# Modulation vectors of layer 1 and of keys/values: column pairs replaced by whole matrix rows, and all weights in one packed tensor

## The chip, the cores and the metric

One core of a Trainium2 chip runs the whole program. The metric is device time in microseconds (us), median of three runs. TensorE (PE) multiplies matrices, VectorE (DVE), ScalarE (ACT) and GpSimd (POOL) work on tiles of 128 partitions, and SyncE (SP) issues the loads, which 16 DMA engines carry out.

## The reference

A decoder trunk of two layers on 256 positions of width 1024, all in float32. Every sub-layer normalizes its input and then modulates it with vectors computed from one condition vector `c`:

```python
cs = jax.nn.silu(c)
shift, scale, gate = jnp.split(cs @ mod_w[layer] + mod_b[layer], 3, axis=-1)
h = _modulate(_rmsnorm(x, norm_g[layer]), shift, scale)   # h * (1 + scale) + shift
# layer 0: u, g = split(h @ w_in); conv of width 4; two gates; scan; y * silu(g); @ w_out
# before layer 1, keys and values from the residual x after layer 0:
shift, scale = jnp.split(cs @ kv_mod_w + kv_mod_b, 2, axis=-1)
h = _modulate(_rmsnorm(x, kv_norm_g), shift, scale)
k, v = jnp.split(h @ w_kv, 2, axis=-1)
# layer 1: q, g = split(h1 @ w_in); causal attention inside one block; o * silu(g); @ w_out
x = x + gate[:, None, :] * y
```

The products of `cs` with the modulation matrices are vector by matrix: for layer 1's shift and scale, and for those of keys and values, a matrix of 1024 x 2048 (8 MB) is read once each, and 2048 numbers come out.

## The kernel before, in words

**Weights.** Every weight comes in blocks of 512 KB into a ring of 11 raw buffers (`NRAW`), in the order of the table `ORDER`. A block takes the buffer of the block 11 places ahead of it, once all users of that one are done. Names: `s`, `m0` are modulation of layer 0 (`m0h` shift, `m0c` scale), `mk` of keys/values, `m1` of layer 1, `g0`/`g1` the gates; `wu`, `wga`, `wgc` the input projection of layer 0, `wo` its output; `wv`, `wka`, `wkb` values and keys; `wgb`, `wqa`, `wqb` gate path and queries of layer 1; `wp` its output.

**Float32 products.** A weight block is split into a high and a low part (`_hi` by a cast on ACT or DVE, `_lo` by a subtraction on DVE), as is the activation, and three fast products (hi·hi, hi·lo, lo·hi) replace one exact one (`mm3`).

**Modulation.** `mod_pair` takes two tiles of 128 outputs at once (a "pair"). `gemv` runs four products at a time, one in each quadrant of 32 columns of the array: shift and scale, even and odd rows, with `cs` repeated over 32 columns (`csB`) as the stationary side. For `mk` all eight row tiles go through PE: 4 rounds of 4 products for a pair. For `m1` row tiles 2 to 7 are summed on DVE (`mac`, `ON_DVE`) and the sum goes through PE with a stationary side of ones: 2 rounds. The profile counts every one of these float32 products as two MATMULs. The row vectors then go to SBUF (`part`, a copy), become columns by two products with `sel2` (`mc`), and get bias and gain on DVE (`sg4`); `mod_apply` uses them on `x1T`, the transposed normalized x.

**The order of the work.** All instructions are recorded and `Plan` places them engine by engine with a list schedule on rough costs, with random changes to the priorities that are kept where its planned end does not suffer. Each engine then runs its list in order. So any change of costs or of program text can move instructions anywhere. Around the change the sequence is: output projection of layer 0 (`r_wo`, lines 851 to 883), residual and root mean square (`resid`, `rms`, `xn_b`), transposition (`tp_b` to `x1T`), `mod_apply` with `mk`, values and keys (`v`, `k`, `pj_wkb`), `mod_apply` with `m1`, gate path and queries (`g`, `q`, `pj_wqb`), attention, output projection (`r_wp`).

Of the kernel before, what the change touches and what calls it, by code (L numbers as in the profile page):

```python
# [44 lines left out]
class Plan:  # L45
    """Records a program and issues it in the order of a list schedule.

    Instructions are recorded in program order with the regions they read and write; what
    they must wait for follows from that and from the buffers of each tag.  They are then
    placed engine by engine by the length of work that still hangs on them, with rough  # L50
    costs, and issued in the order of their planned starts."""
# [109 lines left out]
        # the buffers of a tag are taken over in turn, once all uses of the last tile are done  # L161
# [47 lines left out]
    # a list schedule: of what can start about now, each engine takes what is most urgent  # L209
    def _forward(self, urge):  # L210
# [12 lines left out]
        while len(seq) < n:  # L223
# [61 lines left out]
    def order(self):  # L285
# [14 lines left out]
        # shaken priorities are kept where they do no harm  # L300
# [51 lines left out]
def kernel(ctx: ExitStack, tc: tile.TileContext, x, c, mod_w, mod_b, norm_g,  # L352
                       rg_w_in, rg_conv_w, rg_conv_b, rg_w_a, rg_b_a, rg_w_x, rg_b_x,
                       rg_lambda, rg_w_out, kv_norm_g, kv_mod_w, kv_mod_b, w_kv,
                       att_w_in, att_w_out, final_norm_g, out):
# [17 lines left out]
    w_in, w_out = rg_w_in[0], rg_w_out[0]  # L373
    aw_in, aw_out = att_w_in[0], att_w_out[0]

    # ------------------------------------------------------------------ streamed loads
    def rows(w, kt0, n):
        return w[kt0 * P:(kt0 + n) * P, :].rearrange("(k p) n -> p k n", p=P)

    def cols(w, c0, n):  # L380
        return w[:, c0:c0 + n].rearrange("(k p) n -> p k n", p=P)

    loads = []

    def want(name, shape, *src):
        loads.append((name, shape, src))

    def want_cols(nm, w, c0, qs=(0, 1)):
        for q in qs:
            want(f"{nm}_{q}", [P, 4, 256], cols(w[q * 512:(q + 1) * 512], c0, 256))  # L390

    def want_rows(nm, w, k0=0, k1=KT):
        for k in range(k0, k1):
            want(f"{nm}_{k}", [P, D], w[k * P:(k + 1) * P, :])

    def want_pair(nm, w, i):
        want(f"{nm}_{i}", [P, 2, 512], rows(w, 2 * i, 2))

    def want_out(nm, w, qs=(0, 2)):
        for q in qs:  # L400
            for n in range(2):
                for r in (q, q + 1):
                    want_pair(f"{nm}{n}", w[:, n * 512:(n + 1) * 512], r)

    def want_mod(nm, w, i):
        for q in range(2):
            for x, c0 in (("h", 0), ("c", D)):
                want_cols(f"{nm}{x}{i}", w, c0 + i * 256, (q,))

    def want_block(b):  # L410
        nm, i = b[:-1], int(b[-1])
        if nm == "s":
            want(f"m0h0_{i}", [P, KT, P], cols(mod_w[0], i * P, P))
            want(f"m0c0_{i}", [P, KT, P], cols(mod_w[0], D + i * P, P))
        elif nm in ("m0", "m1"):
            want_mod(nm, mod_w[i_of[nm]], i)
        elif nm == "mk":
            want_mod(nm, kv_mod_w, i)
        elif nm in ("wu", "wv", "wgb"):
            w, c0 = {"wu": (w_in, 0), "wv": (w_kv, D), "wgb": (aw_in, D)}[nm]  # L420
            want_rows(nm, w[:, c0:c0 + D], i, i + 1)
        elif nm in ("wga", "wka", "wqa"):
            w, c0 = {"wga": (w_in, D), "wka": (w_kv, 0), "wqa": (aw_in, 0)}[nm]
            want_pair(nm, w[:, c0:c0 + 512], i)
        elif nm in ("wgc", "wkb", "wqb"):
            w, c0 = {"wgc": (w_in, D), "wkb": (w_kv, 0), "wqb": (aw_in, 0)}[nm]
            want_cols(f"{nm}{i}", w, c0 + 512 + i * 256)
        elif nm in ("gax", "wgax"):
            want(b, [P, 4, 256], *(w[0, i].rearrange("(k p) n -> p k n", p=P) for w in (rg_w_a, rg_w_x)))
        elif nm in ("g0-", "g1-"):  # L430
            want_rows(nm[:2], mod_w[int(nm[1])][:, 2 * D:], 4 * i, 4 * i + 4)
        else:
            want_out(nm, {"wo": w_out, "wp": aw_out}[nm], (2 * i,))

    i_of = {"m0": 0, "m1": 1}
    for b in ORDER.split():
        want_block(b)
    weights = [l[0] for l in loads if l[0][0] == "w"]
# [629 lines left out]
```

## Time and profile before

| | us |
|---|---|
| median of three runs | 271.81 (271.41 to 272.17) |
| span of the profiled execution, first to last instruction | 269.5 |
| PE busy | 254.6 (94%) |
| DVE busy | 212.2 (79%) |
| ACT busy | 145.6 (54%) |
| read from HBM | 70.87 MB |

The profile has no total of its own for the profiled execution beside the span; the median of the runs is 2.3 us above that span. In the views below, all times count from the first instruction. A row of the chain of waits is a piece of the path that ended last; a row of the timeline is an instruction, or several alike in a row.

### The profile page before, as it was taken

To read this page: it belongs to the slowest core of one execution; us is meant where nothing else is said; L and a number is where in the kernel's file an instruction comes from. 1 tells how busy PE (TensorE), PEld (TensorE's weight loads), DVE (VectorE), ACT (ScalarE), POOL (GpSimd) and SP (SyncE) were. 2 spreads that over 40 slices of the span, in tenths; PEclk is the share of its full clock that TensorE was granted. 3 is DMA by queue.
4 is the path that set the end of the run, shared out by engine and by line. 5 is a ranking of instruction groups with operands and counts; after the bars stand their busy time and mean duration, and the time that the engine had idled before them with its cause. 6 is when DMAs were issued, how large, how long until landed. Compare 5 with 4: busy or idle time off the path is not lost.

```text
span 269.5 us, 5236 instructions
## 1 busy us (share of the span) xinstructions
PE 254.6 (94%) x1987; PEld 222.9 (83%) x1987; DVE 212.2 (79%) x427; ACT 145.6 (54%) x278; POOL 18.2 (7%) x31
## 2 busy tenths in 40 slices
PE   8788999999999799989999999999999999999980
PEld 8675887999799586866887898898899999888870
DVE  3652873869988999897677995997777999998783
ACT  7531740778599793585322252764163629894142
POOL 8100000000030200000000000000010000006120
PEclk9999999999999999999999999999999999999996
DMA  6999999998599985769979999899999692000003
GB/s 210 313 351 379 362 366 384 358 406 322 180 333 358 371 257 182 273 183 349 334 244 359 348 279 306 290 304 389 359 391 378 195 362 88 1 4 1 0 13 142
DMA packets 50968, 72.26 MB, mean 268 GB/s; under 512 B 2792, under 2 KB 37888, under 8 KB 50944
## 3 DMA queue, kind: packets, MB, share of 16 engines
q1 hardware_dynamic: 50112, 71.15, 78.1%
q0 software_dynamic: 688, 0.59, 0.7%
q8 instruction: 15, 0.25, 0.4%
q10 hardware_dynamic: 144, 0.20, 0.2%
q14 instruction: 9, 0.07, 0.1%
HBM read 70.87 MB, written 1.05 MB: 267 GB/s over the span
## 4 chain that ended last, share of the span: by engine, by line
PE 83%; SPq 5%; DMA 4%; DVE 4%; ACT 2%; issue 1%; DVEq 0%
PE g L332 9%; PE v L332 8%; PE r_wo L332 8%; PE r_wp L332 8%; PE u L332 7%; SPq L332 5%; PE pj_wkb L332 4%; PE k L332 4%; PE pj_wgc L332 4%; PE pj_wqb L332 4%; PE q L332 4%; PE ga L332 4%; DMA wga<-in_rg_w_in_dram 4%; PE gvm L332 3%; PE gvmk L332 3%; PE sc L332 2%
## 5 line engine op out<-in xcount | busy, mean ns | idle before, releaser
L332 PE MATMUL g<-h_hi,wgb_hi 128*128 128x256 f32 x64 | 18.4, 288 | 0.0
L332 PE MATMUL g<-h_lo,wgb_hi 128*128 128x256 f32 x64 | 18.3, 287 | 0.0
L332 PE MATMUL g<-h_hi,wgb_lo 128*128 128x256 f32 x64 | 18.1, 283 | 0.0
L332 PE MATMUL u<-h_lo,wu_hi 128*128 128x256 f32 x64 | 18.1, 291 | 0.0
L332 PE MATMUL u<-h_hi,wu_lo 128*128 128x256 f32 x64 | 17.8, 286 | 0.0
L332 ACT ACT_TABLE_LOAD x13 | 16.7, 1283 | 0.9 <-PEq L1054 0.7
L94 ACT COPY partm<-gvm 128x256 f32<-128x256 f32 x7 | 2.6, 373 | 26.0 <-PE gvm L332 26.0
L332 PE MATMUL u<-h_hi,wu_hi 128*128 128x256 f32 x64 | 15.9, 284 | 0.7 <-ACT h_hi L94 0.7
L332 PE MATMUL r_wp<-wp_hi,o_hi 128*128 128x512 f32 (+1 forms) x40 | 14.3, 356 | 0.0
L332 PE MATMUL r_wp<-wp_lo,o_hi 128*128 128x512 f32 (+1 forms) x40 | 14.2, 355 | 0.0
L332 PE MATMUL r_wo<-wo_hi,y_hi 128*128 128x512 f32 x32 | 12.6, 397 | 1.6 <-ACT y_hi L94 1.6
L332 PE MATMUL r_wp<-wp_hi,o_lo 128*128 128x512 f32 (+1 forms) x40 | 14.1, 351 | 0.0
L332 PEld LDWEIGHTS u<-h_lo,wu_hi 128*128 128x128 f32 x64 | 12.2, 190 | 1.8 <-issue 1.8
L332 PEld LDWEIGHTS g<-h_hi,wgb_hi 128*128 128x128 f32 x64 | 12.2, 191 | 1.2 <-issue 0.8
L332 PE MATMUL v<-wv_hi,hk_hi 128*128 128x512 f32 x32 | 12.9, 404 | 0.0
L332 PE MATMUL v<-wv_lo,hk_hi 128*128 128x512 f32 x32 | 12.6, 395 | 0.0
L332 PE MATMUL r_wo<-wo_hi,y_lo 128*128 128x512 f32 x32 | 12.4, 394 | 0.0
L332 PE MATMUL r_wo<-wo_lo,y_hi 128*128 128x512 f32 x32 | 12.3, 390 | 0.0
L332 PE MATMUL v<-wv_hi,hk_lo 128*128 128x512 f32 x32 | 12.3, 390 | 0.0
L332 PEld LDWEIGHTS g<-h_hi,wgb_lo 128*128 128x128 f32 x64 | 12.3, 192 | 0.0
L332 PEld LDWEIGHTS g<-h_lo,wgb_hi 128*128 128x128 f32 x64 | 12.2, 191 | 0.0
L332 PEld LDWEIGHTS u<-h_hi,wu_lo 128*128 128x128 f32 x64 | 12.2, 191 | 0.0
(308 smaller groups left out, 897.2 us busy)
## 6 DMA issues: line engine op xcount, KB each, us to landing
g<-in_mod_w_dram SPq DMA_DIRECT2D x16, 512.0 KB, 7.6
m0h<-in_mod_w_dram SPq DMA_DIRECT2D x8, 512.0 KB, 9.6
m0c<-in_mod_w_dram SPq DMA_DIRECT2D x8, 512.0 KB, 9.9
wu<-in_rg_w_in_dram SPq DMA_DIRECT2D x8, 512.0 KB, 8.8
wo<-in_rg_w_out_dram SPq DMA_DIRECT2D x8, 512.0 KB, 7.9
mkh<-in_kv_mod_w_dram SPq DMA_DIRECT2D x8, 512.0 KB, 7.0
mkc<-in_kv_mod_w_dram SPq DMA_DIRECT2D x8, 512.0 KB, 6.6
wv<-in_w_kv_dram SPq DMA_DIRECT2D x8, 512.0 KB, 4.7
```

What stands on the lines that cost most here:

```text
L94: self.record(eng, fn, args, kw, lambda f=f, args=args, kw=kw: f(*args, **kw))
L332: self.plan.record(self.name, fn, args, kw, lambda: f(*args, **kw))
```

## The change

Both modulations are computed from whole rows of the matrix. A block now holds one row tile (128 rows) of the shift or the scale matrix with all 1024 columns. `Rows.quads` sends it through PE in four products, one for each quadrant; quadrant a takes the columns whose place in a group of 128 is 32a to 32a+31, so that the moving side reads 8 pieces of 32 numbers. Shift fills the first 256 columns of one PSUM bank, scale the other 256. Row tiles 2 to 4 of `mk` and 0 to 5 of `m1` are summed on DVE, 1024 columns wide, before PE sees the sum. At the end one transposition of 32x32 blocks on DVE (`V.transpose`) turns the bank into columns: the copy, the `sel2` products and the steps by pair are gone. The matrices `mk` and `m1` are loaded earlier. The host lays all blocks out one after the other in one tensor `pack`, so that each load of 512 KB moves 128 pieces of 4 KB; before, the pieces were of 512 bytes (`s`), 1 KB (`m0`, `mk`, `m1`, `wgc`, `wkb`, `wqb`, `gax`, `wgax`), 2 KB (`wga`, `wka`, `wqa`, `wo`, `wp`) or 4 KB (`wu`, `wv`, `wgb`, `g`).

```diff
-    wgc0 wgax0 wgax1 g0-0 g0-1 wgc1 gax2 gax3 wo0 mk0 wo1 mk1
-    wv0 wv1 wv2 wv3 wka0 mk2 wka1 mk3 wv4 wv5 wka2 wv6 wv7 wka3 wkb0 m10 wkb1 m11
-    wgb0 wgb1 wqa0 m12 wgb2 wgb3 wqa1 m13 wgb4 wgb5 wqa2 wgb6 wgb7 wqa3 wqb0 wqb1 g1-0 g1-1 wp0 wp1
+    wgc0 wgax0 wgax1 g0-0 g0-1 wgc1 gax2 gax3 mk0 mk1 wo0 mk2 mk3 mk4 wo1 mk5 mk6 mk7
+    wv0 wv1 wv2 wv3 wka0 m10 wka1 m11 wv4 wv5 wka2 m12 m13 wv6 wv7 m14 wka3 m15 wkb0 m16 m17 wkb1
+    wgb0 wgb1 wqa0 wgb2 wgb3 wqa1 wgb4 wgb5 wqa2 wgb6 wgb7 wqa3 wqb0 wqb1 g1-0 g1-1 wp0 wp1
-ON_DVE = {"m1": range(2, KT), "g1": range(KT)}
+ON_DVE = {"mk": range(2, 5), "m1": range(6), "g1": range(KT)}
...
-            for i, sc in enumerate(src):
-                SP.dma_start(t if len(src) == 1 else t[:, 2 * i:2 * i + 2], sc)
+            SP.dma_start(t.rearrange("p k n -> p (k n)") if len(shape) == 2 else t, pack[i])
...
-            plan.join(first, n / 0.6 + 83)
+            plan.join(first, n / 0.6 + 108)
...
+    class Rows:
+        def quads(self, st, tiles, last):
+            for w, t in enumerate(tiles):
+                first = len(plan.ops)
+                for a in range(4):
+                    PE.matmul(self.gv[32 * a:32 * a + 32, w * 256:(w + 1) * 256], st,
+                              t.rearrange("p (m q c) -> p q m c", q=4, c=32)[:, a],
+                              start=(not self.begun and w == 0), stop=last,
+                              tile_position=(0, 32 * a), skip_group_check=True)
+                plan.join(first, 256 / 0.6 + 108)
+            self.begun = True
+        def rows(self, *kts):
+            for kt in kts:
+                tiles = [got[f"{self.nm}{w}_{kt}"] for w in "hc"]
+                if kt not in self.dve:
+                    self.quads(csB[:, kt], tiles, kt == KT - 1)
+                    continue
+                for t, acc in zip(tiles, self.accs):
+                    if not self.fresh:
+                        plan.scale(acc, t, csT[:, kt:kt + 1])
+                    else:
+                        V.scalar_tensor_tensor(acc, t, csT[:, kt:kt + 1], acc, ALU.mult, ALU.add)
+                self.fresh = True
+        def total(self):
+            self.quads(ones[:, 0:32], self.accs, False)
+        def finish(self, gain, bias):
+            gT = tmp.tile([P, 512], F32, tag="gT", name=f"gT{self.nm}", bufs=1)
+            V.transpose(gT, self.gv)
+            t4 = const.tile([P, KT, 2], F32, name=f"cols{self.nm}")
+            V.tensor_add(t4, gT.rearrange("p (w m c) -> p m w c", w=2, c=32)[:, :, :, 0], bias)
+            V.tensor_mul(t4[:, :, 1], t4[:, :, 1], gain)
...
-    colsk = [mod_pair("mk", i, *argsk) for i in range(KPRE)]
+    modk = Rows("mk", bank)
+    modk.rows(0, 1)
+    # out_rows("wo", ...) with modk.rows(2, 3, 4) between its halves
+    modk.total()
+    modk.rows(5, 6, 7)
+    colsk = modk.finish(*argsk)
...
-        if i + KPRE < 4:
-            colsk.append(mod_pair("mk", i + KPRE, *argsk))
+        mod1.rows(*((0,), (1,), (2, 3), (4, 5))[i])
...
-        cols1.append(mod_pair("m1", i, *args1))
+        if i == 0:
+            mod1.total()
+            mod1.rows(6, 7)
+    cols1 = mod1.finish(*args1)
```

The planner's costs change a little (13 instead of 2 ns on a fast product, 390 instead of 360 bytes per ns for loads), and the DMA scratch area is set to 4096 bytes.

The first place is PE's list from the end of the output projection of layer 0 to the transposition of x1. `mc_mk` are the `sel2` products, `gvmk` the quadrant products, `macmkh` and `macmkc` the sums made on DVE. Before:

```order
L332 MATMUL mc_mk_395<-sel_222,partmk_394 128x2 x2
L332 MATMUL gvmk_397<-mkh_0_139,csB 32x256 x2
L332 MATMUL gvmk_397<-mkc_0_140,csB 32x256 x2
L332 MATMUL gvmk_397<-mkh_0_139,csB 32x256 x2
L332 MATMUL gvmk_397<-mkc_0_140,csB 32x256 x2
L332 MATMUL gvmk_397<-mkh_1_141,csB 32x256 x2
L332 MATMUL gvmk_397<-mkc_1_142,csB 32x256 x2
L332 MATMUL gvmk_397<-mkh_1_141,csB 32x256 x2
L332 MATMUL gvmk_397<-mkc_1_142,csB 32x256 x2
L332 MATMUL mc_mk_399<-sel_222,partmk_398 128x2 x2
L332 MATMUL tp_b_412<-ident,xn_b_411 128x128 x4
```

and now:

```order
L399 MATMUL r_wo_379<-wo_3_hi,y_lo 128x512
L399 MATMUL gvmk<-macmkh,ones 32x256 x4
L399 MATMUL gvmk<-macmkc,ones 32x256 x4
L399 MATMUL gvmk<-mkh_145,csB 32x256 x4
L399 MATMUL gvmk<-mkc_146,csB 32x256 x4
L399 MATMUL gvmk<-mkh_147,csB 32x256 x4
L399 MATMUL gvmk<-mkc_148,csB 32x256 x4
L399 MATMUL gvmk<-mkh_149,csB 32x256 x4
L399 MATMUL gvmk<-mkc_150,csB 32x256 x4
L399 MATMUL tp_b_409<-ident,xn_b_408 128x128 x4
L399 MATMUL tp_b_410<-ident,xn_b_408 128x128 x4
```

The 16 products of the pair become 32 here, with the sum of DVE first; the `mc_mk` products are gone, and no `gvmk` stands in the `v` and `k` stages that follow.

The second place is DVE's list at the end of the same projection: `wo_..._lo` are the last splits of its weights, `x_372<-r_wo` the residual. Before:

```order
L332 TENSOR_TENSOR wo_2_lo<-wo_2_137,wo_2_hi 128x1024
L332 TENSOR_TENSOR wo_3_lo<-wo_3_138,wo_3_hi 128x1024
L332 TENSOR_TENSOR x_372<-r_wo_373,gate_g_357 128x512
L332 TENSOR_TENSOR x_372<-x_372,xr 128x512
L332 TENSOR_TENSOR x_372<-r_wo_374,gate_g_357 128x512
L332 TENSOR_SCALAR rb_b_404<-ss_b_403,neps 128x1
```

and now:

```order
L399 TENSOR_TENSOR wo_2_lo<-wo_2_143,wo_2_hi 128x1024
L399 TENSOR_TENSOR wo_3_lo<-wo_3_144,wo_3_hi 128x1024
L399 SCALAR_TENSOR_TENSOR macmkc<-mkc_138,csT,macmkc 128x1024
L399 SCALAR_TENSOR_TENSOR macmkh<-mkh_139,csT,macmkh 128x1024
L399 SCALAR_TENSOR_TENSOR macmkc<-mkc_140,csT,macmkc 128x1024
L399 TENSOR_TENSOR x_372<-r_wo_376,gate_g_357 128x512
L399 TENSOR_TENSOR x_372<-r_wo_377,gate_g_357 128x512
L399 TENSOR_TENSOR x_372<-r_wo_378,gate_g_357 128x512
L399 TENSOR_TENSOR x_372<-x_372,xr 128x512 x2
```

Three of the six sums for `mk` now stand between the last weight split and the residual; the other three instructions of the sums stand earlier in the list, ahead of the second half's scan.

## Rows read from the trace of the kernel before

**Rows 1.** The page, parts 1 and 2: busy us and share, busy tenths of 40 slices.

```profile
PE 254.6 (94%) x1987; PEld 222.9 (83%) x1987; DVE 212.2 (79%) x427; ACT 145.6 (54%) x278; POOL 18.2 (7%) x31
PE   8788999999999799989999999999999999999980
```

**Rows 2.** Chain of waits in order of time: start us, us, what.

```profile
14.71 10.22 DMA wga<-in_rg_w_in_dram
...
26.96 2.65 PE ga L332 x20
...
91.75 11.21 PE r_wo L332 x48
102.96 1.00 PE gvmk L332 x16
...
115.44 0.34 PE mc_mk L332 x4
115.78 1.93 PE gvmk L332 x32
...
118.16 0.61 PE mc_mk L332 x4
...
140.99 1.86 PE gvmk L332 x32
...
165.99 0.99 PE gvm L332 x12
...
174.36 1.03 PE g L332 x7
...
175.73 5.02 PE g L332 x41
...
204.13 5.76 PE g L332 x48
```

**Rows 3.** Stretches: from:to, us, busy us (instructions) of each engine, PEclk, DMA share, GB/s.

```profile
11.90:13.30 1.40, 1.40 (x16) 1.40 (x14) 1.36 (x4) 1.11 (x3) 0.00 (x0) 1.00 1.21 290
17.00:20.00 3.00, 3.00 (x27) 3.00 (x27) 2.22 (x5) 1.01 (x2) 0.00 (x0) 1.00 1.09 351
55.00:58.00 3.00, 3.00 (x28) 3.00 (x27) 1.23 (x3) 2.33 (x4) 0.00 (x0) 1.00 1.03 404
92.00:115.50 23.50, 23.46 (x115) 18.23 (x115) 22.51 (x34) 16.43 (x29) 0.00 (x0) 1.00 0.73 239
121.00:174.40 53.40, 53.40 (x390) 44.83 (x390) 42.25 (x77) 20.52 (x40) 0.00 (x0) 1.00 0.96 314
204.00:247.00 43.00, 43.00 (x319) 39.69 (x318) 39.01 (x81) 28.09 (x71) 3.17 (x5) 1.00 0.42 144
```

**Rows 4.** Timeline of PE: start us, us, instruction, idle before and its releaser.

```profile
91.75 0.50 PE L332 MATMUL r_wo<-wo_hi,y_hi 128*128 128x512 f32 x1 [1.64 <-ACT y_hi L94]
120.84 0.48 PE L332 MATMUL v<-wv_hi,hk_hi 128*128 128x512 f32 x1
```

**Rows 5.** Groups of instructions: busy us, mean ns of one, idle before.

```profile
L332 DVE SCALAR_TENSOR_TENSOR macm<-m1h,csT,macm 128x256 f32<-128x256 f32 x20 | 9.6, 481 | 1.8 <-ACT macm L94 1.7
L332 DVE SCALAR_TENSOR_TENSOR maccg<-g,csT,maccg 128x1024 f32<-128x1024 f32 x7 | 9.0, 1283 | 0.1
L94 DVE CAST wo_hi<-wo 128x1024 fp32r<-128x1024 f32 x5 | 3.3, 686 | 0.0
L332 DVE TENSOR_TENSOR x<-r_wo,gate_g 128x512 f32<-128x512 f32 x4 | 2.8, 689 | 0.8 <-PE r_wo L332 0.8
```

**Rows 6.** Timeline of DVE, columns as in Rows 4.

```profile
24.95 0.69 DVE L94 CAST wga_hi<-wga 128x1024 fp32r<-128x1024 f32 x1 [5.57 <-DMA wga<-in_rg_w_in_dram]
109.01 0.68 DVE L332 TENSOR_TENSOR x<-r_wo,gate_g 128x512 f32<-128x512 f32 x1
117.32 0.75 DVE L94 TENSOR_SCALAR xn_b<-x,ry_b 128x1024 f32<-128x1024 f32 x1
120.18 1.22 DVE L332 TENSOR_TENSOR wv_lo<-wv,wv_hi 128x1024 fp32r<-128x1024 f32 x1
```

More of the change, by code (lines that the diff above doesn't have):

```diff
@@ new lines, with blocks, want, cols @@
+    wgb0 wgb1 wqa0 wgb2 wgb3 wqa1 wgb4 wgb5 wqa2 wgb6 wgb7 wqa3 wqb0 wqb1 g1-0 g1-1 wp0 wp1
+"""
+ON_DVE = {"mk": range(2, 5), "m1": range(6), "g1": range(KT)}
+def blocks():
+    out = []
+    def want(name, shape, *src):
+        out.append((name, shape, src))
+    def cols(nm, w, c0, qs=(0, 1)):
+        for q in qs:
+            want(f"{nm}_{q}", (4, 256), (*w, q * 512, 512, c0, 256))
+    def pair(nm, w, i, c0):
+        want(f"{nm}_{i}", (2, 512), (*w, i * 256, 256, c0, 512))
+    for b in ORDER.split():
+        nm, i = b[:-1], int(b[-1])
+        if nm == "s":
+            for x, c0 in (("h", 0), ("c", D)):
+                want(f"m0{x}0_{i}", (KT, P), ("mod_w", 0, 0, D, c0 + i * P, P))
+        elif nm == "m0":
+            for q in range(2):
+                for x, c0 in (("h", 0), ("c", D)):
+                    cols(f"m0{x}{i}", ("mod_w", 0), c0 + i * 256, (q,))
+        elif nm in ("m1", "mk"):
+            w = {"m1": ("mod_w", 1), "mk": ("kv_mod_w", None)}[nm]
+            for x, c0 in (("h", 0), ("c", D)):
+                want(f"{nm}{x}_{i}", (D,), (*w, i * P, P, c0, D))
+        elif nm in ("wu", "wv", "wgb"):
+            w, c0 = {"wu": (("rg_w_in", 0), 0), "wv": (("w_kv", None), D), "wgb": (("att_w_in", 0), D)}[nm]
+            want(b[:-1] + f"_{i}", (D,), (*w, i * P, P, c0, D))
+        elif nm in ("wga", "wka", "wqa"):
+            w, c0 = {"wga": (("rg_w_in", 0), D), "wka": (("w_kv", None), 0), "wqa": (("att_w_in", 0), 0)}[nm]
+            pair(nm, w, i, c0)
+        elif nm in ("wgc", "wkb", "wqb"):
+            w, c0 = {"wgc": (("rg_w_in", 0), D), "wkb": (("w_kv", None), 0), "wqb": (("att_w_in", 0), 0)}[nm]
+            cols(f"{nm}{i}", w, c0 + 512 + i * 256)
+        elif nm in ("gax", "wgax"):
+            want(b, (4, 256), *((w, (0, i), 0, 256, 0, 256) for w in ("rg_w_a", "rg_w_x")))
+        elif nm in ("g0-", "g1-"):
+            for k in range(4 * i, 4 * i + 4):
+                want(f"{nm[:2]}_{k}", (D,), ("mod_w", int(nm[1]), k * P, P, 2 * D, D))
+        else:
+            w = {"wo": ("rg_w_out", 0), "wp": ("att_w_out", 0)}[nm]
+            for n in range(2):
+                for r in (2 * i, 2 * i + 1):
+                    pair(f"{nm}{n}", w, r, n * 512)
+    return out
@@ new lines, with packed @@
+BLOCKS = blocks()
+def packed(inputs):
+    import numpy as np
+    out = np.empty((len(BLOCKS), P, D), np.float32)
+    for b, (_, shape, srcs) in zip(out, BLOCKS):
+        at = 0
+        for name, layer, r0, nr, c0, nc in srcs:
+            a = inputs[name] if layer is None else inputs[name][layer]
+            part = a[r0:r0 + nr, c0:c0 + nc].reshape(-1, P, nc).transpose(1, 0, 2).reshape(P, -1)
+            b[:, at:at + part.shape[1]] = part
+            at += part.shape[1]
+        assert at == D
+    return out
@@ L202, in _tails @@
                 if o["fn"] == "dma_start" and not real:
-                    gap = max(o["cost"], o["bytes"] / 360)
+                    gap = max(o["cost"], o["bytes"] / 390)
                 else:
@@ L263, in _forward @@
             if o["fn"] == "dma_start":
-                queue = max(queue, t + (1100 if e == "sync" else 1700)) + o["bytes"] / 360
+                queue = max(queue, t + (1100 if e == "sync" else 1700)) + o["bytes"] / 390
                 fin[i] = queue
@@ L351, with kernel @@
 @with_exitstack
[L352 to L355, printed above, removed]
+def kernel(ctx: ExitStack, tc: tile.TileContext, x, c, mod_b, norm_g, rg_conv_w, rg_conv_b,
+                       rg_b_a, rg_b_x, rg_lambda, kv_norm_g, kv_mod_b, final_norm_g, pack, out):
     nc = tc.nc
@@ L372 @@
     x, c, out = x[0], c[0], out[0]
[L373 to L438, printed above, removed]
+    weights = [b[0] for b in BLOCKS if b[0][0] == "w"]
     windex = {n: i for i, n in enumerate(weights)}
@@ L848, with out_rows @@
             split_into(sg[:, sl], y_h[:, sl], y_l[:, sl])
-    def out_rows(name, hh, hl, done, pieces):
+    def out_rows(name, hh, hl, done, pieces, between=lambda: None):
         bs = [bank(f"r_{name}{i}") for i in range(len(pieces))]
@@ L868, in out_rows @@
                 go(n, (2 * r, 2 * r + 1), range(ST))
+        between()
         for n in range(2):
```

41 lines of the change are left out of this document (21 added, 20 removed).

## The prediction

> **What bounds the kernel now.** I read the page first: PE is busy for 94% of the span, every other engine less, and the tenths are 9 nearly everywhere [rows 1]. So a change counts if it takes work from PE or closes one of the few gaps of PE, and not otherwise. The chain of waits says where PE's unbroken run begins: it reaches back to a load, that of the first `wga` block, issued at 14.71 [rows 2]; DVE had been idle for 5.57 us when that block landed, and split it from 24.95 [rows 6]. From there to the end of the last projection the chain is PE with one real gap, the 1.64 us before `r_wo` [rows 4], where the scan of layer 0 runs. The stretches tell the same: 53.40 of 53.40 us busy in the key and value stage, 43.00 of 43.00 in attention [rows 3]. But in the stretch of `r_wo`, 92 to 115.5, DVE is busy for 22.51 of 23.50 us beside PE's 23.46 [rows 3]: there two engines are full at once, and what the change adds on DVE in this stretch can't be free.
>
> The numbers below are for the profiled execution, span 269.5 us; the median of the runs, 271.81, is 2.3 above it, and I carry a difference over one to one.
>
> **The change part by part. 1: quadrant products.** 32 MATMULs of `gvmk` in one piece take 1.93 us [rows 2], 0.060 each. Before, `mk` has 128 of them (4 pairs x 16 products x 2 MATMULs); 16 stand in the scan's gap and cost nothing, 112 are on the path: 6.7 us. `m1` has 4 pairs of 12 MATMULs at 0.99 us [rows 2]: 4.0. The eight `mc` steps at 0.34, of which one took 0.61 with its wait [rows 2], are 3.0. Together 13.7. Now `mk` has 6 row tiles (five and the sum) x 2 matrices x 4 quadrants x 2 = 96 MATMULs, of which the order puts 32 into the scan's gap: 16 more than before, 0.96 us, under the cover of the 1.64 us of waiting there, so nothing. 64 are left on the path, 3.8 us, all right behind `r_wo`. `m1` has 3 x 2 x 4 x 2 = 48 in one piece, 2.9 us. 13.7 - 6.7 = 7.0 saved. The same small steps also broke up the big products: 48 of `g` take 5.76 us undisturbed, and 1.03 + 5.02 = 6.05 around an `mc` [rows 2], 0.29 more. Some six of seven such places go; I take 1.5 of the 1.7 us. **Saved: 8.5.** The trace before has no moving side in strided pieces on PE, so the price per MATMUL is bounded from below by the 0.060 (fewer columns are not read) and from above by 0.99/12 = 0.083, the dearest group of the same form [rows 2]; the 112 left would then cost 9.3 instead of 6.7. I take 0.060, since that is the row with whole runs of rounds, as the new order has them.
>
> **2: DVE around `r_wo`.** New here are two scalings of 128x1024 (nearest: a cast of that size, 0.69 us) and four sums of that size (1.28 us, the `maccg` row): 6.5 us [rows 5]. Two of the five casts of `wo` go to ACT, 1.4 less; a cast of `y_hi` comes to DVE and one `sg` step moves in, some 1.0. Net about 6. The residual starts at 109.01 without having waited for PE [rows 6], so DVE is late there already; it now starts at about 115. Four multiplications and four additions at 0.69 [rows 5] are 5.5 us, and some small steps of the norm follow; I take 5.7, so that `xn_b` starts at about 120.7 instead of 117.32 [rows 6]: 3.4 late. From `xn_b` to the first `v` it is 3.5 us (117.32 to 120.84, [rows 4, 6]), nothing in that part changes, so `v` starts 3.4 late, at about 124.2. PE has its 64 MATMULs meanwhile, to about 120.9, and then waits some 2 us. Behind `xn_b` all four `wv_lo` splits (1.22 each [rows 6]) now stand on DVE between the small steps, about 1.7 us for a row tile where PE needs 1.4: 1.3 us more. The 32x32 transposition is not in the trace; it reads a 128x512 bank once, like the residual's multiplication (0.69), or twice (1.4); it stands behind `xn_b` of the first half, where it delays only the second half, and for `m1` the second `pj_wkb` covers it. I take 0.7. **Lost: 4.7**; bounds 0 (the sums fit into waits for ACT and PE) and 8 (all 6.5 on the path and the splits queued behind).
>
> The `m1` sums: before 2 x 20 steps at 0.481 [rows 5] and 8 scalings, now 10 at 1.28 and 2 scalings: 19 to 14 us on DVE, but all before the end of the first `pj_wkb`. DVE was busy for 42.25 of 53.40 us there [rows 3]; my count of the new list from `xn_b` to the last sum is 35 us against 40 of PE. Covered; if that cover is gone, what is missing comes one to one on PE's wait for `macm1h`.
>
> **3: the start.** With 512-byte pieces the engines moved 290 GB/s (11.9 to 13.3), with 1 KB 351 (17 to 20), with 4 KB 404 (55 to 58), all at a full DMA share [rows 3]. Ahead of the first `wga` stand four `s` blocks (2.1 MB: 7.2 us at 290, 5.2 at 404) and four `m01` blocks (6.0 to 5.2): 2.8 us, so that `wga` is there about 22.2 instead of 24.95. The `s1` blocks, which the second quadrant products and so half of `u` need, gain the first 2.0 of it. The piece of `ga` that ended the wait ran from 26.96 for 2.65 us, to 29.6 [rows 2]; it moves with `wga` as long as PE's own work ahead of it moves too, and since that follows closely I take a little less. **Saved: 2.4**, bounds 0 and 4. Later blocks gain the same 0.8 each four, so the loads stay ahead of PE. The Trainium skill, "DMA: Bandwidth & Descriptors", section Specifications, gives 512 bytes as the least transfer for line rate; by that the packing would bring nothing and the sum would be 2.4 higher. The 290 against 404 GB/s speak against it.
>
> **4: the middle of layer 0.** Casts of `wgc` and `wgax` move from ACT to DVE where the convolution's steps queue; PE's fillers (`gvg`) are cut up between the gate products. I take 0.4 lost, bounds -0.5 and 1. Attention has its DVE sums of `g1` moved ahead, out of a stretch in which PE waits for nothing [rows 3]: no gain.
>
> **Sum:** -8.5 + 4.7 - 2.4 + 0.4 = -5.8: span 263.7, median 271.81 - 5.8 = **266.0**.
>
> **Rivals.** (a) The wait ahead of `v` doesn't come, since DVE's sums slip into the waits for ACT's square root and `xn_b` is late by under 1 us: another 4 us, about 262, down to 260. For it: DVE in 92 to 115.5 is only full by an order that can be packed anew. Against: 0.99 us of idle time is all there is [rows 3].
> (b) Packing brings nothing, as PE's own work on `u` and the quadrant products is the bound of the start: 268.4. For it: PE is busy from 17 to 20 without a gap [rows 3]. Against: the chain runs through the load [rows 2].
> (c) The wait takes all: the buffers of `mk` 3 and 4 are freed only by the three late sums, the next loads (`mk7`, `wv`) wait for these in the ring, and `wv` lands at 122 to 123; `v` then runs 7 to 8 us late, and the sum is 269.5 to 271.5. For it: the three sums stand last ahead of the residual. Against: `wv` needs four blocks of 1.3 us each at 404 GB/s.
> (d) Slower: the moving side in pieces of 32 columns, 128 columns apart, halves the rate of the quadrant products. Then 112 MATMULs cost 13.4 instead of 6.7, and the 32 in the scan's gap 3.8 instead of 1.9, of which 0.7 are covered: 266.0 + 6.7 + 1.2 = 273.9. It decides from a price of about 0.11 us each. For it: no row shows such a read. Against: four products share the time, and each still gives 256 columns. The Trainium skill, "SBUF — State Buffer", section on the two sides, says that reads within a 16-byte line run at full bandwidth; a piece of 128 bytes is eight whole lines, so by that there is no such price; no run here shows it yet.
>
> **Chances.** Forecast 0.54 (its own range 263.5 to 268); (a) 0.14; (b) 0.14; (c) 0.12, of which 0.05 within 0.3% (271.0 to 272.6, about what a measurement of this kernel can tell from no change); (d) 0.06. Faster: 0.54 + 0.14 + 0.14 + 0.07 = 0.89; same 0.05; slower 0.06. Range 261.5 to 270: below it lies half of (a), above it (d) and most of (c).
>
> **What would show it.** Step 1: `gvmk` in the chain as one piece of 64 MATMULs behind `r_wo` with 3.8 us, `gvm` as one of 48 with 2.9, no `mc_mk`. Step 2: an idle time of PE of 1 to 3 us ahead of `tp_b` or `v`, released by `xn_b`; the first residual on DVE directly behind the three sums, without a wait for PE. Step 3: the first `ga` ends at about 27.2 instead of 29.6, GB/s near 400 in the first slices. Wrong would be: quadrant products above 0.083 us each, no earlier `ga`, or PE waiting in the `k` stage for `wka` or before `g` for `h`.

## The result, and the profile after

The changed kernel takes 263.52 us (262.91 to 264.42), the one before 271.88 beside it; the ratio is 0.9697, 95% interval 0.9676 to 0.9719. Predicted were 266.0 in a range of 261.5 to 270.0. The span of the profiled execution went from 269.5 to 261.5.

The page of the changed kernel, to be read against [rows 1]:

```profile
span 261.5 us, 5044 instructions
PE 249.1 (95%) x1923; PEld 219.6 (84%) x1923; DVE 215.0 (82%) x393; ACT 140.1 (54%) x265; POOL 17.1 (7%) x31
PEclk9999999999999998899999999999999999999998
GB/s 225 412 417 420 414 421 416 422 336 164 343 355 270 248 396 293 220 288 338 414 405 390 416 417 271 288 401 313 280 333 325 234 0 3 0 1 1 3 1 160
```

Two things stand out. The first slices move 412 to 422 GB/s where before the same slices stood at 313 to 384. And PEclk has two 8s, at 98 to 111 us, where before has nines everywhere but in its last slice: a cost that the prediction didn't have.

Where the time went is read best from a few milestones on PE (us, each from its own trace's first instruction; minus is earlier):

| | before | after | change so far |
|---|---|---|---|
| first piece of `ga` ends | 29.62 | 26.22 | -3.4 |
| second `pj_wgc` ends | 82.20 | 79.87 | -2.3 |
| `r_wo` starts | 91.75 | 88.58 | -3.2 |
| second half of `r_wo` starts | 103.89 | 101.85 | -2.0 |
| `r_wo` ends | 115.44 | 115.12 | -0.3 |
| `v` starts | 120.84 | 122.18 | +1.3 |
| `g` and `q` end | 212.77 | 205.28 | -7.5 |
| `r_wp` ends | 261.73 | 254.27 | -7.5 |

So three things happen: the start wins 3.4, everything from there to `v` loses 4.7, and behind `v` 8.8 are won. The chain of waits of after (start, length, engine, what, count) shows the first and the last, against [rows 2]:

```profile
15.36 5.26 PE u L399 x43
...
88.31 6.96 DMA wo<-in_pack_dram
...
96.35 1.07 ACT aq L399
97.45 1.24 DVE wgx L399
98.71 1.34 DVE aq L399 x3
101.85 13.28 PE r_wo L399 x48
...
133.87 5.75 PE k L399 x48
...
162.06 2.73 PE gvm L399 x48
...
170.73 5.76 PE g L399 x48
```

No load stands in the start any more; `g`, `k` and `pj_wkb` run in whole pieces of 48; `gvm` is one piece of 48 with 2.73 us (the prediction had 2.9). And `r_wo` has become two pieces with something between: ACT's square root (`aq`) and the scan. The load of `wo` that the chain puts ahead of `aq` isn't what held it: ScalarE works from 88.69 to 99.30 without a gap. The timeline of PE in this place (start, length, tile, count; in brackets the wait and who ended it), against [rows 4]:

```profile
99.65 0.39 PE L399 MATMUL r_wo<-wo_hi,y_lo 128*128 128x512 f32 x1
101.85 0.50 PE L399 MATMUL r_wo<-wo_hi,y_hi 128*128 128x512 f32 x1 [1.81 <-ACT y_hi L161]
...
104.53 0.63 PE L399 MATMUL r_wo<-wo_lo,y_hi 128*128 128x512 f32 x1
104.96 0.63 PE L399 MATMUL r_wo<-wo_hi,y_lo 128*128 128x512 f32 x1
...
115.05 0.64 PE L399 MATMUL gvmk<-macmkh,ones 128*32 128x256 f32 x8
115.50 0.61 PE L399 MATMUL gvmk<-macmkc,ones 128*32 128x256 f32 x8
...
118.83 1.09 PE L399 MATMUL tp_b<-ident,xn_b 128*128 128x128 f32 x8
121.12 1.06 PE L399 MATMUL tp_b<-ident,xn_b 128*128 128x128 f32 x8 [1.20 <-ACT hrmk L161]
122.18 0.50 PE L399 MATMUL v<-wv_hi,hk_hi 128*128 128x512 f32 x1
```

Eight quadrant MATMULs stand 0.43 to 0.45 apart, 0.054 each. Behind the wait of 1.81 the products of `r_wo` stand 0.43 apart (104.53 to 104.96); ahead of it and from 106 on it is 0.23. The windows say why (the columns are the stretch, its length, PE busy with its instructions, the granted clock, the DMA share and GB/s):

```profile
99.00:101.80 2.80, 1.03 (x5) 1.00 0.91 373
101.80:103.00 1.20, 1.15 (x3) 0.80 0.09 38
103.00:104.00 1.00, 1.00 (x2) 0.50 0.49 160
104.00:105.00 1.00, 1.00 (x4) 0.50 0.93 369
...
106.00:107.00 1.00, 1.00 (x6) 1.00 0.73 274
```

The granted clock is 0.50 there, the lower of its two levels (1.2 of 2.4 GHz), for about 3.5 us behind the wait. In before 16 `gvmk` MATMULs stood in this place (from 102.89) and no wait, and the clock stayed at 1.00. VectorE in the same stretch, against [rows 6]:

```profile
107.99 1.27 DVE L399 SCALAR_TENSOR_TENSOR macmkc<-mkc,csT,macmkc 128x1024 f32<-128x1024 f32 x1
...
110.39 1.27 DVE L399 SCALAR_TENSOR_TENSOR macmkc<-mkc,csT,macmkc 128x1024 f32<-128x1024 f32 x1
111.58 1.87 DVE L399 TENSOR_TENSOR x<-r_wo,gate_g 128x512 f32<-128x512 f32 x3
...
115.15 0.69 DVE L399 TENSOR_TENSOR x<-r_wo,gate_g 128x512 f32<-128x512 f32 x1 [0.50 <-PE r_wo L399]
...
118.03 0.75 DVE L161 TENSOR_SCALAR xn_b<-x,ry_b 128x1024 f32<-128x1024 f32 x1
...
119.07 0.70 DVE L399 STREAM_TRANSPOSE gTmk<-gvmk 128x512 f32<-128x512 f32 x1
...
120.23 0.75 DVE L161 TENSOR_SCALAR xn_b<-x,ry_b 128x1024 f32<-128x1024 f32 x1
```

The residual starts at 111.58 right behind the sums, as the prediction said, and 2.6 later than before. But at 115.15 VectorE waits for PE again, so the lateness is gone by then. In before it was much the same: only the first piece of the residual had not waited for PE, two others had, 0.8 together in [rows 5], and the last piece starts as `r_wo` ends (115.44):

```profile
110.94 0.69 DVE L332 TENSOR_TENSOR x<-r_wo,gate_g 128x512 f32<-128x512 f32 x1 [0.52 <-PE r_wo L332]
...
115.47 0.69 DVE L332 TENSOR_TENSOR x<-r_wo,gate_g 128x512 f32<-128x512 f32 x1
```

### The profile page after: what moved, and what is told of

Read it like the earlier page. It is cut to its first block, busy times and chain, and to the rows that moved or that the text cites. A ratio compares the mean times of both kernels' runs of the same rounds, so it can differ in the third digit from the quotient of the medians.

```text
span 261.5 us, 5044 instructions
## 1 busy us (share of the span) xinstructions
PE 249.1 (95%) x1923; PEld 219.6 (84%) x1923; DVE 215.0 (82%) x393; ACT 140.1 (54%) x265; POOL 17.1 (7%) x31
## 4 chain that ended last, share of the span: by engine, by line
PE 86%; DVE 7%; DMA 3%; ACT 2%; issue 1%; ACTq 0%
PE u L399 9%; PE g L399 9%; PE v L399 8%; PE r_wp L399 6%; PE r_wo L399 5%; PE ga L399 5%; PE pj_wgc L399 4%; PE pj_wkb L399 4%; PE pj_wqb L399 4%; PE q L399 4%; PE k L399 4%; PE gvm L399 3%; DMA wo<-in_pack_dram 3%; PE pa L399 3%; PE sc L399 3%; PE px L399 2%
## 5 line engine op out<-in xcount | busy, mean ns | idle before, releaser
L399 PE MATMUL u<-h_hi,wu_hi 128*128 128x256 f32 x64 | 18.4, 287 | 0.0
L399 PE MATMUL r_wo<-wo_hi,y_hi 128*128 128x512 f32 x32 | 13.6, 424 | 1.8 <-ACT y_hi L161 1.8
L399 PE MATMUL r_wo<-wo_lo,y_hi 128*128 128x512 f32 x32 | 13.0, 407 | 0.0
L399 PE MATMUL r_wo<-wo_hi,y_lo 128*128 128x512 f32 x32 | 13.0, 412 | 0.0
L399 PEld LDWEIGHTS u<-h_hi,wu_hi 128*128 128x128 f32 x64 | 12.2, 191 | 0.6 <-issue 0.6
L399 POOL DMA_DIRECT2D row_g<-gsg x8 | 3.9, 497 | 129.0 <-ACT aq L399 68.1
```

The lines of the kernel that those rows point to most:

```text
L399: self.plan.record(self.name, fn, args, kw, lambda: f(*args, **kw))
```

## The experiments

In seven of the twelve (`e_pack`, `e_rows`, `e_contig`, `e_nosum`, `e_fill`, `e_fillnosum`, `e_twice`) the order of every engine was held fast, so that only the named thing differs; in the others the planner set it anew. Times stand against 271.9 us for the kernel before in each set of runs.

**Packing alone** (`e_pack`), on the kernel before:

```diff
-            for i, sc in enumerate(src):
-                SP.dma_start(t if len(src) == 1 else t[:, 2 * i:2 * i + 2], sc)
+            SP.dma_start(t.rearrange("p k n -> p (k n)") if len(shape) == 2 else t, pack[i])
```

> The kernel before with packed weights alone; every engine's order of instructions is that of before. Theory: the pieces of 4 KB (2 KB for the four blocks of wgax and gax) make the loads ahead of the first wga faster, at about 415 GB/s instead of 290 to 350, as in the trace of the changed kernel. The first ga ends at 26.2 to 27 instead of 29.6, and as PE has no other wait until r_wo, r_wo starts about 3 earlier too, if the scan ahead of it moves along: 268.9 (268.3 to 269.8). Rival, PE's own work bounds the start (rival b of the prediction): 271.9. Rival, the 3.4 us seen at the first ga of the changed kernel came from the new order of PE and not from the loads: between 270.5 and 271.9.

Measured: 269.40 us (269.34 to 269.61), ratio 0.9905 (0.9893 to 0.9918), so 2.55 us. The first `ga` piece ends at 27.78, 1.8 earlier; it now waits for nothing of its own, and ahead of it PE works on `mc_m`:

```profile
24.13 0.61 PE L397 MATMUL mc_m<-sel,partm 128*128 128x2 f32 x4 [0.52 <-ACT partm L159]
...
24.66 0.36 PE L397 MATMUL ga<-h_hi,wga_hi 128*128 128x256 f32 x1
```

Packing is worth its 2.55 us. Of the 3.4 at the first `ga` of the changed kernel it gives 1.8 by itself; the rest needs the new order as well.

**Rows without packing** (`e_rows`), the changed kernel with the loads of before:

```diff
-            SP.dma_start(t.rearrange("p k n -> p (k n)") if len(shape) == 2 else t, pack[i])
+            for j, (nm, layer, r0, nr, c0, nc_) in enumerate(src):
+                m = full[nm] if layer is None else full[nm][layer]
...
+                SP.dma_start(t if len(src) == 1 else t[:, 2 * j:2 * j + 2], m)
```

> The changed kernel with its weights loaded from their own tensors again, in pieces of 512 bytes to 4 KB; every engine's order is that of the changed kernel, only the loads differ. Theory: the start loses again what packing gave, 2.4 to 3.4 us, and nothing else changes: 266.5 (265.7 to 267.2). Rival, the packing is worth nothing by itself: 263.5. Rival, the faster loads are also needed in the stage of keys and values, where mk and m1 rows were moved ahead of wv: 268 or more, with waits of PE for wv or wka.

Measured: 266.58 us (265.26 to 267.44), ratio 0.9796 (0.9773 to 0.9819): 3.06 more than the changed kernel, as the theory had it. Its stretches 11.9 to 13.3 and 17 to 20 move 355 and 379 GB/s, against 421 and 418 with packing (the columns are those of [rows 3]):

```profile
11.90:13.30 1.40, 1.40 (x15) 1.37 (x15) 1.37 (x4) 1.34 (x3) 0.00 (x0) 1.00 1.17 355
17.00:20.00 3.00, 3.00 (x28) 3.00 (x27) 1.89 (x5) 1.01 (x2) 0.00 (x0) 1.00 1.09 379
```

In before the same stretches, with pieces of the same sizes, stood at 290 and 351 [rows 3]; what makes that difference wasn't traced. The two parts add up: 2.55 and 5.3 (271.9 - 266.58) are 7.9 of the 8.4 measured together. Without packing the second `pj_wgc` ends at 82.21, where it ended before (82.20), while its first `ga` ends 1.1 earlier: the new plan loses 1.1 in the middle of layer 0.

**Contiguous quadrants** (`e_contig`):

```diff
-                              t.rearrange("p (m q c) -> p q m c", q=4, c=32)[:, a],
+                              t[:, a * 256:(a + 1) * 256],
```

> The changed kernel, where each quadrant product of mk and m1 reads 256 neighbouring columns instead of 8 pieces of 32; the order of all engines is the same. It leaves the outputs in other places, so the modulation of keys, values and layer 1 is computed with permuted vectors. Theory: the strided read costs nothing: eight MATMULs start 0.43 us apart in both, 263.5 (263.0 to 264.0). Rival, the strided read has a price that hides in the 0.43: eight take 0.40 or less, and the 112 MATMULs on the path give back 0.5 us or more: under 263.0.

Measured: 263.47 us (263.06 to 264.07). The rows of the piece are the same to the hundredth:

```profile
116.05 0.61 PE L399 MATMUL gvmk<-macmkc,ones 128*32 128x256 f32 x8
116.48 0.61 PE L399 MATMUL gvmk<-mkh,csB 128*32 128x256 f32 x8
```

The strided read costs nothing.

**Without VectorE's sums of `mk`** (`e_nosum`): the four additions are left out of the program, but planned, so that nothing else moves; the two scalings stay.

```diff
+                        if self.nm == "mk":
+                            plan.ops[-1]["call"] = lambda: None
```

> The changed kernel without the four sums of row tiles 3 and 4 of mk on VectorE (4.9 us of work); it leaves these two row tiles out of the modulation of keys and values. The order of everything else is the same. Rival, as the prediction had it: these sums delay the residual, so without them the residual starts 3.6 earlier and v at least 1.2 to 2.5 earlier: 261.0 to 262.3. Theory after the trace of the changed kernel: the small steps of the first half's norm stand on VectorE behind the last residual piece, which waits for PE until 115.15, and the 64 quadrant products keep PE until 118.8 anyway; so the residual starts earlier but xn_b by 0.5 at most and v by 0.5 at most: 263.3 (262.9 to 263.7).

Measured: 263.63 us (263.30 to 264.14): nothing. VectorE's rows show it:

```profile
108.37 0.69 DVE L399 TENSOR_TENSOR x<-r_wo,gate_g 128x512 f32<-128x512 f32 x1 [0.37 <-PE r_wo L399]
...
115.09 0.69 DVE L399 TENSOR_TENSOR x<-r_wo,gate_g 128x512 f32<-128x512 f32 x1 [0.82 <-PE r_wo L399]
...
117.97 0.75 DVE L161 TENSOR_SCALAR xn_b<-x,ry_b 128x1024 f32<-128x1024 f32 x1
```

The residual starts 3.2 earlier, and then waits for PE, four times; `xn_b` is 0.06 earlier. So the prediction's reason for the late `v` falls, for this order of VectorE's list: the order itself was planned with the sums in it, and it stays here.

**The piece of `m1` cut** (`e_cut`): four pieces of 8 MATMULs inside the first `pj_wkb` (`between` is called there after each row tile), 16 behind it.

```diff
+                between(4 * q + k)
...
-            mod1.total()
-            mod1.rows(6, 7)
+            mod1.quads(ones[:, 0:32], mod1.accs, True)
```

> The changed kernel, where the one piece of 48 quadrant products of m1 is cut: four pieces of 8 stand inside the first pj_wkb, 16 stay behind it. PE's work is the same, with four more changes between quadrant and full products. Theory: a change there and back costs 0.33 us (in the trace of before 16 gvmk between two k cost 1.20, of which 16 x 0.054 = 0.87 are the products), so 4 x 0.33 = 1.3 more: 264.8 (264.3 to 265.3). Rival: the changes cost 0.1 each or less, and the saving behind v has another source: 263.5 to 264.0.

Measured: 265.30 us (264.37 to 265.96), 1.8 more. In its trace `pj_wkb` with its pieces lasts from 157.03 to 172.92, 15.89 us, against 14.58 (156.14 to 170.72): 1.31 for four more pieces, 0.33 each, to the hundredth what the rows of before gave. The rest lies ahead of it: in the profiled execution `pj_wkb` starts 0.9 later already.

**All of `m1` on VectorE** (`e_m1dve`):

```diff
-ON_DVE = {"mk": range(2, 5), "m1": range(6), "g1": range(KT)}
+ON_DVE = {"mk": range(2, 5), "m1": range(8), "g1": range(KT)}
...
-            mod1.total()
             mod1.rows(6, 7)
+            mod1.quads(ones[:, 0:32], mod1.accs, True)
```

> The changed kernel with all eight row tiles of m1 summed on VectorE: 32 MATMULs less on PE, four sums of 1.28 us more on VectorE. Theory: VectorE's last m1 sum ends at 154.7 now and PE asks for it at 162.06, so 5.1 us fit; 32 x 0.054 = 1.7 less: 261.8 (261.3 to 262.3). Rival: the sums of the last two tiles wait for their loads or push the wkb and wgb splits behind them, and PE waits for them: 263.5 to 266.

Measured: 261.89 us (261.55 to 262.37), ratio 0.9618 (0.9590 to 0.9646). `pj_wkb` and its two pieces take 13.19 instead of 14.58: 1.73 for 32 MATMULs less, 0.33 back, since the plan put the two remaining pieces apart. VectorE's cover held. In its profiled execution another 0.5 comes at `v` (121.63 against 122.18), since behind the wait of 1.81 the clock stayed at 1.00.

**All of `mk` on PE** (`e_mkpe`):

```diff
-ON_DVE = {"mk": range(2, 5), "m1": range(6), "g1": range(KT)}
+ON_DVE = {"m1": range(6), "g1": range(KT)}
...
-    modk.total()
```

> The changed kernel with no sums of mk on VectorE: all eight row tiles go through PE as quadrant products, tiles 2 to 4 of them between the two halves of r_wo. VectorE loses two scalings and four sums (6.5 us), PE gets 48 - 16 = 32 MATMULs more (1.7 us), 48 of them in the place where PE now waits 1.8 us for y_hi, and 48 instead of 64 stand behind r_wo. Theory: VectorE's sums cost nothing now, so nothing comes back from there; PE's 2.6 us in the 1.8 us of waiting push the end of r_wo by 0.8 or less, the shorter piece behind it gives 0.9 back to the transposition: 263.5 (262.5 to 264.3). Rival, the prediction's: the sums delay the residual and v, and without them v comes 2 us or more earlier: 261.5 or less.

Measured: 264.20 us (263.47 to 264.64), not told apart from 263.5. The planner moved much else: PE now waits 2.36 us for `y_hi` ahead of the first half of `r_wo`, the clock is 0.50 for some 3.5 us behind that wait, and `v` starts at 123.62. What the missing sums may have given back can have gone there, so this run doesn't decide.

**Two more row tiles between the halves of `r_wo`** (`e_wait`):

```diff
-             lambda: modk.rows(2, 3, 4))
+             lambda: modk.rows(2, 3, 4, 5, 6))
...
-    modk.rows(5, 6, 7)
+    modk.rows(7)
```

> The changed kernel with the quadrant products of mk row tiles 5 and 6 (32 MATMULs, 1.7 us) between the two halves of r_wo instead of behind it. Theory: PE waits there for y_hi for 1.8 us and in short stalls behind it, so r_wo ends when it does now; behind it 32 products are left, PE is through with them by 117, and the 32x32 transposition no longer stands between the two xn_b on VectorE; the second xn_b and so v come 0.7 to 1.2 earlier: 262.6 (262.2 to 263.0). Rival: the tiles land too late and r_wo is pushed: 264 or more. Rival: the residual of the second half sets v alone, and nothing is won: 263.5.

Measured: 265.36 us (263.81 to 266.78): a miss. The planner held the tiles for late and put their products as four single pieces into the second half, and the wait ahead of it stayed:

```profile
102.18 1.19 PE L399 MATMUL r_wo<-wo_hi,y_hi 128*128 128x512 f32 x4 [2.16 <-DVE y_hi L161]
...
103.75 0.64 PE L399 MATMUL gvmk<-mkh,csB 128*32 128x256 f32 x8
```

In the profiled execution (263.81, the shortest of six) `v` stands at 122.24, as in the changed kernel, and the clock stayed at 1.00 behind the 2.16. What the others lost isn't in a trace; their mean clock was 0.978 to 0.987 against 0.992.

**The wait filled, with the sums and without** (`e_fill`, `e_fillnosum`): 32 MATMULs with a stationary side of zeros between the halves of `r_wo`.

```diff
+                nc.tensor.matmul(modk.gv[32 * a:32 * a + 32, 0:256], nil, csB.rearrange("p k n -> p (k n)"),
+                                 start=False, stop=False, tile_position=(0, 32 * a), skip_group_check=True)
```

> The changed kernel with 32 more MATMULs (16 quadrant products with a stationary side of zeros, which add nothing) between the two halves of r_wo, where PE waits 1.8 us for y_hi; every engine's order is else the same. In the trace of the changed kernel the granted clock is 0.50 from 103 to 105 behind that wait, and r_wo's MATMULs start 0.43 to 0.47 apart there instead of 0.23. Theory: work in the wait keeps the clock at 1.00, r_wo ends up to 1.7 us earlier (113.4), but the three sums of mk on VectorE end at 111.7 only and the residual follows them, so v comes 0.5 us earlier at most: 263.0 (262.5 to 263.5). Rival, PE alone sets v: 261.8. Rival, the clock falls for another reason than the wait: no change, 263.5 or a little more.

> The same with the four sums of row tiles 3 and 4 of mk on VectorE left out as well (these two row tiles are left out of the modulation of keys and values). Theory: the half clock and VectorE's sums hide each other: each alone gives 0 to 0.5 us back, both together 1.5 to 1.7, since then neither the end of r_wo nor the residual is late: 261.9 (261.5 to 262.4). Rival: v hangs on a third thing, the transposition and the second xn_b, and both together give no more than the filled wait alone: 263.0 or more.

Measured: 263.45 us (263.32 to 263.91) and 263.38 (263.05 to 263.58). The windows of `e_fill` (columns as in the windows above):

```profile
99.00:101.80 2.80, 2.80 (x35) 1.00 1.02 411
101.80:103.00 1.20, 1.20 (x14) 1.00 0.48 188
...
104.00:105.00 1.00, 1.00 (x5) 1.00 0.94 369
```

With work in the wait the clock stays at 1.00, and `r_wo` takes 25.45 us instead of 26.54: the half clock costs 1.1. `e_m1dve`, where the wait of 1.81 stands unfilled and the clock stayed at 1.00 all the same, takes as long (25.5); its window, columns as above:

```profile
103.00:104.00 1.00, 0.78 (x3) 1.00 0.60 180
```

So the wait doesn't always bring the half clock: of the seven traces with this wait unfilled (1.77 to 1.81 us) six have it, and neither of the two with it filled. `v` comes only 0.6 earlier after the start of `r_wo` (33.03 instead of 33.60), and 1.0 with the sums out as well (32.57), and none of that can be told in the times. I had expected 1.5 to 1.7 from both: this theory fell, and its rival stands, a third thing behind `r_wo`. (`e_fillnosum` leaves two row tiles out of the modulation, as `e_nosum` does.)

**The transposition twice** (`e_twice`):

```diff
+                once = plan.ops[-1]["call"]
+                plan.ops[-1]["call"] = lambda: (once(), once())[1]
```

> The changed kernel with the 32x32 block transposition of mk done twice (0.70 us more on VectorE); every engine's order is else the same. v starts 7.06 us after the end of r_wo now, against 5.40 before. Theory: the transposition stands on VectorE between the two xn_b, can't begin before the 64 quadrant products are through, and the second xn_b, the second tp_b and v follow it, so doubling it puts v 0.64 later behind r_wo (7.7 us): 264.1 (263.7 to 264.5). Rival: v hangs on the transposition of x1 and on the splits alone, the 0.70 is hidden, 7.06 and 263.5 stay.

Measured: 265.13 us (264.47 to 265.45), 1.6 more, where 0.64 were expected. PE and its windows:

```profile
118.86 1.09 PE L399 MATMUL tp_b<-ident,xn_b 128*128 128x128 f32 x8
121.91 1.06 PE L399 MATMUL tp_b<-ident,xn_b 128*128 128x128 f32 x8 [1.96 <-DVE xn_b L161]
122.74 0.64 PE L399 MATMUL v<-wv_hi,hk_hi 128*128 128x512 f32 x1
```

```profile
121.90:122.90 1.00, 0.99 (x9) 1.00 1.00 401
122.90:124.00 1.10, 1.10 (x4) 0.52 1.04 417
124.00:126.00 2.00, 2.00 (x6) 0.50 1.03 418
126.00:128.00 2.00, 2.00 (x9) 0.91 1.01 379
```

The transposition is on the path: the second `xn_b` and `tp_b` come 0.8 later. The wait of PE grows from 1.20 to 1.96, and behind it the clock falls to 0.50 for the first products of `v`, which without the doubling it did not; `k` starts 1.65 later (135.36 against 133.71). Here a wait that grew by 0.76 cost twice that.

**A better version** (`e_best`): `m1` all on VectorE, only row tiles 2 and 3 of `mk` there, and the products of tiles 4 and 5 moved into the wait by hand.

```diff
-ON_DVE = {"mk": range(2, 5), "m1": range(6), "g1": range(KT)}
+ON_DVE = {"mk": range(2, 4), "m1": range(8), "g1": range(KT)}
...
-             lambda: modk.rows(2, 3, 4))
+             lambda: (half.append(len(plan.ops)), modk.rows(2, 3, 4, 5), half.append(len(plan.ops))))
...
+            for i in seq[:at] + late + rest:
```

> A version meant to be better than the changed kernel: all eight row tiles of m1 are summed on VectorE, only row tiles 2 and 3 of mk are, and the quadrant products of mk row tiles 4 and 5 (32 MATMULs) stand in PE's wait for y_hi, 48 behind r_wo. Theory: 1.7 less from m1, the wait filled with work that has to be done, the clock kept, and one pair of sums less on VectorE: v 1.5 us earlier too: 260.3 (259.5 to 261.2). Rival: the new plan puts y_hi or the scan later by as much, and only the gain of m1 is left: 261.5 to 262.5.

Measured: 261.06 us (260.11 to 261.64), ratio 0.9594 (0.9571 to 0.9617): below both kernels, but its interval overlaps that of `e_m1dve`, so the second part of the idea isn't shown to be worth anything. `v` starts at 121.98, only 0.2 earlier than in the changed kernel, where 1.5 were expected. The wait is filled and the clock kept, but `r_wo` starts 1.1 later, and one of the tiles lands late:

```profile
101.70 0.61 PE L405 MATMUL gvmk<-mkh,csB 128*32 128x256 f32 x8
102.96 0.64 PE L405 MATMUL gvmk<-mkc,csB 128*32 128x256 f32 x8 [0.65 <-DMA mkc<-in_pack_dram]
```

## Why the prediction was right, and where it wasn't

The mechanism was right in its main lines: PE is the bound, small steps on PE go, the start gets earlier, and a part is given back around `r_wo`. The time lies inside the range and inside the likeliest case's own range (263.5 to 268), at its edge; 5.8 us were forecast, 8.3 came.

*Step 1, quadrant products: right, its price made of two errors that cancel.* A MATMUL costs 0.054 and not 0.060; the 0.060 of [rows 2] held a share of an interruption. An interruption costs 0.33 for a quadrant piece (1.31 for four in `e_cut`) and 0.44 for an `mc` step (in before, `k` at 138.24 is followed by the next at 138.72 and 138.92 instead of 138.36 and 138.48), and behind `v` there were 8 and 6, not seven in all. (Around `r_wo` the prediction's prices cancel, 48 products and two `mc` steps against 64 products, 3.8 each, so its 8.5 lies all behind `v`.) So before: 112 x 0.054 + 8 x 0.33 + 6 x 0.44 = 11.3; now 48 x 0.054 + 0.33 = 2.9; saved 8.4, against 8.5. Rival (d) is out by `e_contig`. The Trainium skill, "SBUF — State Buffer", in its section on the two sides, puts repeated reads of one 16-byte line at full bandwidth, so a piece of eight whole lines at no price; with 263.47 against 263.52 the runs agree.

*Step 3, the start: right in size.* 2.4 were predicted for the packing, 2.55 (`e_pack`) and 3.06 (`e_rows`) were measured; rival (b) is out as a whole. At the first `ga`, where the 2.4 were to show, packing alone gave 1.8: from there on PE's own work bounds the start, as (b) had it. By the least transfer for line rate that the Trainium skill gives, in "DMA: Bandwidth & Descriptors", Specifications, packing would have brought nothing; the measurement decides against it for this kernel. That the first `ga` came 3.4 earlier and not 2.4 is the new order, and step 4 gives it back: its 0.4 in the middle of layer 0 were 1.1.

*Step 2, VectorE around `r_wo`: the number at `v` right, its reason wrong.* Predicted was `v` at 124.2 - 2.4 + 0.4 = 122.2; it starts at 122.18. But the step that led there, that the sums make the residual late and the residual makes `xn_b` late, failed: `e_nosum` takes 4.9 us of sums away and gains nothing. I had priced VectorE's work as if it were a chain, and read its first residual piece at 109.01 as late, though [rows 5] gave 0.8 of waiting for PE to the pieces behind it. The sums fill waits for PE (3.8 us of them in `e_nosum`); the small norm steps stand in the list behind the last residual piece, which waits for PE in any case.

What makes `v` late instead, by the milestones: the second half of `r_wo` waits 1.81 for `y_hi`, since ACT's chain to the scan moved by 2.0 only (`aq` at 98.37 and 96.35) while `r_wo` started 3.2 earlier and has no filler left (1.2 lost); the half clock behind that wait (1.1, `e_fill`); 0.6 more in its second half, of which `e_fill` puts 0.2 down to a wait for `y_lo` and the rest is open; and 7.06 us from the end of `r_wo` to `v` instead of 5.40 (1.7).

Of these 1.7, 1.0 lies ahead of the first `xn_b` (2.91 behind the end of `r_wo`, before 1.88): four of the first half's norm steps were done ahead of the last residual piece in before, now all of them stand behind it. The other 0.6 lies between `xn_b` and `v` (4.15, before 3.52), where the prediction had "nothing in that part changes": there the transposition stands, on the path by `e_twice`. PE's 64 products hide beside the norm steps: they end at 118.5, `xn_b` starts at 118.03. Whether the sums pushed the norm steps back in the planner's list wasn't tried: `e_nosum` keeps the list. In `e_best`, with none of the sums behind the last weight split and a new list, the first `xn_b` starts at 115.48, ahead of the last residual piece, and `v` stands 5.8 behind `r_wo`; in `e_wait` it is 5.5.

That the prediction's number for `v` came out is luck: its `xn_b` was 0.7 too late (118.7 against 118.03), and the 0.6 behind it was missing, since step 2 names 0.7 for the transposition but leaves it out of its total (3.4, 1.3 and 0.7 are 5.4, not 4.7). It also had no gain ahead of `r_wo`, where the 32 products close the wait of 1.64 and 0.8 come back.

*The other rivals.* (a) had the sums hidden, and they are; but the wait ahead of `v` came all the same (1.20, ahead of `tp_b`), and so not its 262. (c) is out: `wv` is split from 115.33 (ScalarE) and 120.90 (VectorE) on without a wait for its load; and its 7 to 8 us instead of 3.4 would have made 269.6 to 270.6, not up to 271.5.

*What was off by size* is behind `v`. The prediction amounts to -7.2 from `v` to the end (-5.8, with `v` 1.4 late), the trace shows -8.8 to the end of `g`. The 1.3 of step 2 for the `wv_lo` splits didn't come: 48 products of `v` take 11.53 instead of 48 x 0.227 = 10.9, 0.6 too long where before had 0.2. That is 0.9. Another 0.8 is in the stages of `pj_wkb` and `g` of before, which are 0.3 and 0.5 longer than their products and pieces at these prices; the cause is open. Beyond that, 0.5 lies behind the last MATMUL (7.2 us from there to the end, before 7.8) and 0.3 in what lies around the span (2.0 instead of 2.3); both are not explained. Together that is, to 0.1, the 2.5 between 266.0 and 263.5.

## What to carry to other kernels

An engine that is busy for 22.5 of 23.5 us isn't thereby the bound: look in its list for the next instruction that waits for the other engine, since work put in ahead of that one is hidden as long as it pushes nothing else behind that one, and take it out once to know. Small steps between big products cost the change there and back beside their work (0.33 us for a piece of 8 quadrant MATMULs that work for 0.43; 0.44 for a whole `mc` step), so count the places and not only the instructions. When an earlier stage gets faster, ask which chain beside it did not (here ACT's square root): PE reaches it early, waits, and can pay for the wait a second time.

## What the runs showed of the hardware

- Behind waits of PE of 1.8 to 2.4 us the granted clock was 0.50 for about 3.5 us: at 102.5 to 106 in the changed kernel, in the same place in `e_rows`, `e_contig`, `e_nosum`, `e_cut` and `e_twice`, at 122.6 to 126.4 in `e_twice` (1.96) and ahead of the first half of `r_wo` in `e_mkpe` (2.36). Behind 1.20 us at 119.9 and the 1.64 us of before it stayed at 1.00. It is not strict: 1.81 in `e_m1dve` and 2.16 in `e_wait` left it at 1.00 too, and in `e_m1dve` `r_wo` ended 1.0 earlier. What decides isn't shown. The four runs of `e_m1dve` took 261.55 and 261.59 us at a mean clock of 0.991, 262.20 and 262.37 at 0.986, so it is likely one source of the spread between runs of one kernel.
- One core loaded 412 to 422 GB/s over seven slices, 45 us, with 4 KB pieces.
- A 32x32 block transposition of a 128x512 bank on VectorE took 0.70 us, as long as one multiplication over it (0.69).
